# Another order around the seven value products of an attention layer

## The chip, the cores and the metric

The kernel runs on one core of a Trainium2 chip. The metric is the device time of one execution in microseconds (us). Times are compared by the median of several runs; the profile page shows one profiled execution. The engines are TensorE (PE, matmuls; its weight loads are listed as PEld), VectorE (DVE), ScalarE (ACT), GpSimd (POOL, which computes and also issues some DMAs) and SyncE (SP, which issues the others). Each engine works through its own queue in order and waits for semaphores of the others. SBUF is the memory that all engines read; PE writes its sums to PSUM, eight banks of 128 x 512 float32.

## The reference

A trunk of two layers over 512 tokens of width 1024. Layer 0 mixes tokens with a gated linear recurrence, layer 1 with stick-breaking attention; each mixer is followed by a SwiGLU block (FFN), and each part has a root-mean-square norm ahead of it. The part that matters here is the start of the attention layer:

```python
h = _rmsnorm(x, norm_mix_g[1])
qkv = (h @ w_qkv).reshape(bsz, s, 3, SB_HEADS, SB_HEAD_DIM)
...
z = einsum("bhqd,bhkd->bhqk", qb, k32) * scale
log_beta = log_sigmoid(z)
log_1m = where(mask, log_sigmoid(-z), 0.0)
suffix = cumsum(log_1m, reverse=True) - log_1m
wts = where(mask, exp(log_beta + suffix), 0.0)
out = einsum("bhqk,bhkd->bhqd", wts, v32)
```

All is float32. The kernel gets this precision from PE by splitting each operand into a rounded high part and a remainder (`h` and `l`) and adding three matmuls: high x high, high x low, low x high.

## The kernel before

**Layout.** `x` is held transposed: eight tiles `x[0..7]` of 128 features x 512 tokens. At the end of the first FFN block (lines 1023 to 1065) its result is turned back by PE in two halves (`back`), `take(m)` adds a turned tile to `x[m]` on DVE, and `gain(m)` makes the attention's operands `u[m] = (uh, ul)`: `x` times the norm's gain, cast on ACT, remainder on DVE (lines 425, 426). `gain` also squares `x[m]` on ACT and adds the square to `acc` (line 481): tiles 1 to 6 on POOL, tile 7 on DVE. The sum over features of `acc`, taken by PE, gives the norm's factor per token (`norm_rs1`, which ends in a small chain of ACT and DVE and writes a diagonal matrix); `norm_rs2` spreads it with PE over a 128 x 512 tile `rsB`. The factor is applied after the projections.

**The value projection** is one matrix product of 512 tokens x 1024 features by 1024 x 1024. It is cut in two along tokens, features and columns, and done with seven block products in place of eight, as in Strassen's scheme (Winograd's variant). `vprod(q, out, c)` (line 559) is one call of product `q`: half `c` of its k tiles, twelve matmuls of 512 columns into two banks. So a product is two calls, 24 matmuls. Products 1, 2 and 4 use `u` itself. Products 5 and 6 use sums made by `vops1(k)`, 7 and 3 sums made by `vops2(k)`, for k = 0 to 3: ACT scales two tiles of `x`, DVE makes sums of 256 columns, ACT casts the high part, DVE subtracts for the low part. Banks: `A` = 4 and 5, `B` = 2 and 3, `B2` = 0 and 1. Between products the banks are copied (ACT) or added (DVE) into `r1`, `u2`, `b5`, and `v_evac` writes value tiles `vs` from them: two ACT and two DVE instructions for each bank, ACT and DVE by turns.

**Weights** come as pieces of 512 KB in a fixed list; `VUnit.order` (line 79) says in which order the seven products' pieces and the first three q/k tiles of weights (`"k"`) stand in it. Each is split by `split_one()`: `wh` by ACT (line 329), `wl` by DVE or POOL (line 331; of the value stage, the list positions in `V_POOL` go to POOL). There are three buffers of `wh` and of `wl`, so a split waits for the matmuls of the third tile before it. `chunk()` hands the next piece to a product or a projection; ahead of that it issues loads on SP and runs `split_one()` until a set distance ahead of the use is reached, three pieces in the value stage. Pieces of products 6, 7 and 4 are not loaded: `plus` adds a second block to the buffer of an earlier piece (5, 3 and 6) with an accumulating DMA that POOL issues (line 101) at the next call of `chunk()` after that piece's split.

**Projections.** `proj(t, part)` is half of tile `t` of queries (even t) or keys (odd t), twelve matmuls. `proj_evac1` scales it on DVE by `rsB`; `proj_evac2` splits it, and for queries SP then copies it with eight DMAs into operands of two heads. `s1(h)` is the scores of head h into three banks (head 0: banks 0 to 2, head 1: banks 3 to 5). `chain_a(h)` follows: three ACT functions, two DVE and one POOL instruction for each of the three banks. `rsum` adds a few DVE steps, `s2(h)` adds the masked sums on PE, `chain_b` and `s3` end the head. From `h = 0` on a loop over heads mixes these with the remaining projections.

**Order.** In a `manual_schedule` block the instructions of PE, ACT, DVE and POOL run in the order in which the code traces them. The end of the FFN and the attention are two such blocks; where they meet, a scheduler interleaves them, and it also places the DMAs of SP. The order around the products before is in lines 1329 to 1397: products 1, 5, 3, 6, 2, 7, then scores and chain of head 0, then product 4.

## Time and profile before

| | |
|---|---|
| three runs | 1117.54, 1118.59, 1120.10 us; median 1118.59 |
| the profiled execution's own time | 1120.09 us |
| its span, first to last instruction | 1118.4 us |
| mean granted PE clock | 0.992 of full speed |
| seven value products, first to last matmul | about 492 to 567 us of the span |

The 1.7 us between span and time lie outside the program's instructions. Rows of a timeline read: start and length in us, engine, line, operation, output<-inputs by the program's names, count; in brackets how long the engine sat idle before it, and who ended the idle time. Matmul lengths overlap; what counts is the distance of their starts. A row with "x4" merges neighbours of one kind.

### The profile page before, as it was taken

What the parts mean: (1) busy time and instruction counts of PE and PEld (TensorE: products, weight loads), DVE (VectorE), ACT (ScalarE), POOL (GpSimd) and SP (SyncE); (2) the same over time, 40 slices, a digit from 0 to 9 for tenths busy, and PEclk for the clock granted to TensorE, in tenths of its full rate; (3) what the DMA queues carried; (4) which work ended last, traced back from release to release, by engine and by line L of the source; (5) the groups of instructions that cost most, each with busy time, mean ns of one, the idle gap of its engine ahead of it and who ended that gap; (6) DMA issues with size and microseconds to landing.
All of it is one profiled execution on the core that took longest, in us unless ns stands there. A gap on an engine that the chain in (4) does not pass through costs nothing.

```text
span 1118.4 us, 14779 instructions
## 1 busy us (share of the span) xinstructions
PE 1088.2 (97%) x5231; PEld 905.7 (81%) x5231; DVE 922.2 (82%) x1285; ACT 729.6 (65%) x1112; POOL 375.3 (34%) x283
## 2 busy tenths in 40 slices
PE   9999999999999999998889999999999999999997
PEld 6888888888888888876668888888887888888895
DVE  7977787777979799987778888978669797988897
ACT  6697677666555564646669999977764554646465
POOL 1652432324242414122434444422232415140412
PEclk9999999999999999999889999999999999999999
DMA  8532349977777765443853342224887767675432
GB/s 312 139 97 76 114 133 218 189 211 155 205 162 184 174 147 147 129 129 61 177 161 83 91 128 78 77 79 131 205 187 183 177 166 191 156 203 115 151 73 75
DMA packets 48537, 164.06 MB, mean 147 GB/s; under 512 B 5840, under 2 KB 6096, under 8 KB 48464
## 3 DMA queue, kind: packets, MB, share of 16 engines
q1 hardware_dynamic: 34640, 113.32, 31.1%
q0 software_dynamic: 13536, 49.29, 25.1%
q8 instruction: 41, 0.67, 0.2%
q10 hardware_dynamic: 288, 0.52, 0.1%
q14 instruction: 32, 0.26, 0.1%
HBM read 152.62 MB, written 2.10 MB: 138 GB/s over the span
## 4 chain that ended last, share of the span: by engine, by line
PE 67%; DVE 13%; ACT 6%; issue 4%; DMA 2%; DVEq 0%; POOL 0%; POOLq 0%; ACTq 0%
PE bank L793 15%; PE bank L794 15%; PE bank L795 15%; PE bank L369 5%; PE bank L367 5%; PE bank L368 5%; DVE wl L331 4%; PE bank L1240 2%; DMA bu<-w_gu 2%; DVE y L785 2%; PE bank L1266 1%; ACT wh L329 1%; PE bank L800 1%; PE bank L568 1%; ACT t L1204 1%
## 5 line engine op out<-in xcount | busy, mean ns | idle before, releaser
L329 ACT CAST wh<-raw 128x1024 fp32r<-128x1024 f32 x130 | 135.8, 1048 | 79.5 <-PE bank L795 34.5
L331 DVE TENSOR_TENSOR wl<-raw,wh 128x1024 fp32r<-128x1024 f32 x112 | 168.7, 1509 | 21.9 <-ACT wh L329 21.8
L793 PE MATMUL bank<-wh,ow 128*128 128x512 f32 (+1 forms) x480 | 179.7, 374 | 1.7 <-DVE b L785 1.7
L795 PE MATMUL bank<-wh,ow 128*128 128x512 f32 (+1 forms) x480 | 178.3, 372 | 0.0
L794 PE MATMUL bank<-wl,ow 128*128 128x512 f32 (+1 forms) x480 | 178.3, 371 | 0.0
L101 POOL DMA_DIRECT2D bu<-w_gu x64 | 56.2, 878 | 274.6 <-DMA bu<-w_gu 125.5
L329 ACT CAST wh<-bu 128x1024 fp32r<-128x1024 f32 x72 | 75.7, 1052 | 64.2 <-PE bank L795 38.3
L331 DVE TENSOR_TENSOR wl<-bu,wh 128x1024 fp32r<-128x1024 f32 x70 | 86.9, 1258 | 29.7 <-ACT wh L329 28.9
L793 PEld LDWEIGHTS bank<-wh,ow 128*128 128x128 f32 x480 | 90.4, 188 | 18.2 <-issue 2.9
L369 PE MATMUL bank<-uh,wl 128*128 128x512 f32 x256 | 100.6, 395 | 4.3 <-DVE wl L331 4.3
L367 PE MATMUL bank<-uh,wh 128*128 128x512 f32 x256 | 102.3, 402 | 2.2 <-ACT wh L677 1.0
L795 PEld LDWEIGHTS bank<-wh,ow 128*128 128x128 f32 x480 | 90.4, 188 | 15.7
L794 PEld LDWEIGHTS bank<-wl,ow 128*128 128x128 f32 x480 | 90.4, 188 | 15.3
L368 PE MATMUL bank<-ul,wh 128*128 128x512 f32 x256 | 100.5, 394 | 0.6 <-DVE ul L426 0.5
L785 DVE TENSOR_TENSOR y<-y,bank 128x512 f32<-128x512 f32 x140 | 88.9, 678 | 2.2 <-PE bank L795 2.1
L793 PE MATMUL bank<-wh,hth 128*128 128x512 f32 (+1 forms) x194 | 75.4, 389 | 0.0
L794 PE MATMUL bank<-wl,hth 128*128 128x512 f32 (+1 forms) x194 | 75.2, 387 | 0.0
L795 PE MATMUL bank<-wh,htl 128*128 128x512 f32 (+1 forms) x194 | 75.1, 387 | 0.0
L331 DVE TENSOR_TENSOR wl<-bv,wh 128x1024 fp32r<-128x1024 f32 x46 | 60.6, 1327 | 17.3 <-ACT wh L329 17.2
L331 POOL TENSOR_TENSOR wl<-raw,wh 128x1024 fp32r<-128x1024 f32 x20 | 50.8, 2543 | 69.6 <-ACT wh L329 57.9
L329 ACT CAST wh<-bv 128x1024 fp32r<-128x1024 f32 x48 | 49.7, 1048 | 22.4 <-PE bank L795 13.5
L369 PEld LDWEIGHTS bank<-uh,wl 128*128 128x128 f32 x256 | 48.6, 190 | 15.1 <-DVE wl L331 4.7
(309 smaller groups left out, 2811.7 us busy)
## 6 DMA issues: line engine op xcount, KB each, us to landing
bu<-w_gu POOLq DMA_DIRECT2D x64, 512.0 KB, 5.6
raw<-w_gu SPq DMA_DIRECT2D x44, 512.0 KB, 3.7
raw<-w_dn SPq DMA_DIRECT2D x24, 512.0 KB, 5.2
bu<-w_gu SPq DMA_DIRECT2D x22, 512.0 KB, 4.3
bv<-w_gu SPq DMA_DIRECT2D x22, 512.0 KB, 4.2
bv<-w_gu POOLq DMA_DIRECT2D x22, 512.0 KB, 6.7
d<-w_dn SPq DMA_DIRECT2D x20, 512.0 KB, 3.6
raw<-w_qk SPq DMA_DIRECT2D x16, 512.0 KB, 3.7
```

The lines of the kernel that those rows point to most:

```text
L101: kern.soon(lambda: kern.nc.gpsimd.dma_start(t, self.part(n), accum_op=ALU.add))
L329: (self.nc.vector.tensor_copy if self.wh_dve else self.nc.scalar.copy)(wh[:, c], raw)
L331: self.wli = self.wl_engine(i).tensor_tensor(wl[:, c], raw, wh[:, c].bitcast(F32), ALU.subtract)
L367: mm(out, lhsT=wh, rhs=xh, start=first, stop=False)
L368: mm(out, lhsT=wh, rhs=xl, start=False, stop=False)
L369: mm(out, lhsT=wl, rhs=xh, start=False, stop=last)
L568: mm(out[j], lhsT=oh[:, ts(j)], rhs=h, start=first and k == 0, stop=False, skip_group_check=True)
L785: add = lambda o, a, b: nc.vector.tensor_tensor(o, a, b, ALU.add)
L793: mm(out, lhsT=xh, rhs=wh, start=first, stop=False, skip_group_check=True)
L794: mm(out, lhsT=xh, rhs=wl, start=False, stop=False, skip_group_check=True)
L795: mm(out, lhsT=xl, rhs=wh, start=False, stop=last, skip_group_check=True)
L1240: mm(zt[kt][:, o0:o0 + ZW[j]], lhsT=tri if j == kt else one_n, rhs=s_, start=False, stop=True, skip_group_check=True)
```

## The change

- `gain` no longer squares. The squares of all eight tiles come behind product 5 (`squares`), and their adds are all on DVE. `norm_rs1` and `norm_rs2` move from around product 5 to around product 6's second call.
- Takes and gains 4 to 7 move from the FFN's block into the attention's block, takes by twos ahead of the gains.
- `vops1` and `vops2` become `scaled`, `ops1` and `ops2`: two k tiles at a time, halves and casts of both first, then both remainders. `ops2` makes the operands of product 3 and of product 7 apart; those of 7 come behind the squares. The full `vl`, `vh` pair of `vops2` becomes one tile per product and k.
- The distance of `chunk()` in the value stage becomes 1, and `split_one()` (`S_`) is called at chosen places. Products 2 and 7 change places in the list. POOL's positions are 12, 14 and 16: the second pieces of 7, 2 and 4.
- The evacuation of the three first projections comes behind the norm: `proj_evac1` for all three, one product call later `proj_evac2`.
- `v_evac` issues its two ACT instructions ahead of its two DVE instructions.
- Product 4's first call and the split of the fourth q/k tile come ahead of the scores and chain of head 0, which stay ahead of product 4's second call and of the last value tiles.

```diff
-V_POOL = (8, 10, 12, 14, 16)
+V_POOL = (12, 14, 16)
...
-        self.order = (1, "k", "k", "k", 5, 3, 6, 2, 7, 4)
+        self.order = (1, "k", "k", "k", 5, 3, 6, 7, 2, 4)
...
-        ahead = ahead or (4 if ffn else 3 if v else self.AHEAD_SPLIT)
+        ahead = ahead or (4 if ffn else 1 if v else self.AHEAD_SPLIT)
...
-                        self.norm_in(m, gnext)
+                        self.norm_in(m, gnext, False)
...
                 take(2, 3)
+                self.split_one()
                 self.vprod(1, self.bank[4:6], 0)
                 gain(2, 3)
+                self.split_one()
                 back(1)
                 self.vprod(1, self.bank[4:6], 1)
-                for m in range(4, KT):
-                    take(m)
-                    gain(m)
+                self.rest = take, gain
...
+                def scaled(k):
                     ua, ub, w1 = w[k] = [self.new("vw") for _ in range(3)]
                     nc.scalar.activation(ua, self.x[k], AF.Copy, scale=self.col("g_mix1", k))
                     nc.scalar.activation(ub, self.x[k + 4], AF.Copy, scale=self.col("g_mix1", k + 4))
...
+                def ops1(*ks):
+                    for k in ks:
+                        ua, ub, w1 = w[k]
+                        sub(w1[:, lo], ub[:, hi], ua[:, hi])
+                        nc.vector.scalar_tensor_tensor(w1[:, hi], w1[:, lo], -1.0, ua[:, lo], ALU.mult, ALU.subtract)
+                        h, l = self.new("vh", F32R), self.new("vl", F32R)
+                        nc.scalar.copy(h, w1)
+                        self.vops[k] = {5: (h[:, lo], l[:, lo]), 6: (h[:, hi], l[:, hi]), 1: (h, l)}
+                    for k in ks:
+                        h, l = self.vops[k][1]
+                        sub(l, w[k][2], h.bitcast(F32))
+
+                def ops2(q, *ks):
+                    for k in ks:
+                        ua, ub, w1 = w[k]
+                        hl = self.new("vx", F32R)
+                        if q == 3:
+                            o = ub[:, hi]
+                            nc.vector.scalar_tensor_tensor(o, ub[:, lo], -1.0, w1[:, hi], ALU.mult, ALU.subtract)
+                        else:
+                            o = ub[:, lo]
+                            sub(o, ua[:, lo], ua[:, hi])
+                        nc.scalar.copy(hl[:, lo], o)
+                        self.vops[k][q] = hl[:, lo], hl[:, hi]
+                        self.vops[k][-q] = o, hl
+                    for k in ks:
+                        h, l = self.vops[k][q]
+                        sub(l, self.vops[k][-q][0], h.bitcast(F32))
+                        if q == 7:
+                            self.rel(*w[k])
...
                         nc.scalar.activation(v[:, :, 0:64], pj, AF.Copy, scale=r)
+                    for j in range(2):
+                        v = vs[t][2 * half + j]
+                        pj = pvv[:, 4 * j:4 * j + 4, :]
                         nc.vector.scalar_tensor_tensor(v[:, :, 64:128], pj, r, v[:, :, 0:64].bitcast(F32),
                                                        ALU.mult, ALU.subtract)
...
+                def squares(*ms):
+                    for m in ms:
+                        self.norm_sq(m, nc.vector)
+
+                take(4)
+                take(5)
+                gain(4)
+                gain(5)
+                take(6)
+                take(7)
                 copies(r1, A)
+                gain(6)
+                gain(7)
                 pq = []
                 for t in range(2):
                     proj(t, 0)
                     pq.append((self.pt, self.pw))
-                    vops1(t)
+                S_()
+                scaled(0)
+                scaled(1)
+                ops1(0, 1)
                 for t in range(2):
                     self.pt, self.pw = pq[t]
                     proj(t, 1)
                 proj(2, 0, self.bank[0])
                 pq.append((self.pt, None))
-                vops1(2)
-                vops1(3)
+                S_()
+                scaled(2)
+                scaled(3)
+                ops1(2, 3)
+                S_()
                 proj(2, 1)
+                ops2(3, 0, 1)
+                self.vprod(5, B, 0)
+                S_()
+                ops2(3, 2, 3)
+                self.vprod(5, B, 1)
+                copies(b5, B)
+                S_()
+                squares(0, 1, 2, 3)
+                self.vprod(3, B, 0, False)
+                S_()
+                squares(4, 5, 6, 7)
+                self.vprod(3, B, 1, False)
+                ops2(7, 0, 1)
+                S_()
+                self.vprod(6, A, 0, False)
                 self.bi = 1
                 self.norm_rs1()
                 nc.vector.tensor_scalar(self.nrs, self.rsT, -1.0, None, ALU.mult)
                 nc.scalar.preload_act_table_set("natural_log_exp_and_others")
...
+                ops2(7, 2, 3)
+                S_()
+                self.vprod(6, A, 1, False)
...
+                copies(u2, A)
                 self.bi = 1
                 self.norm_rs2()
...
+                S_()
+                tts = []
+                for t in range(3):
                     self.pt = pq[t][0]
                     proj_evac1(t)
-                    proj_evac2(t)
...
+                    tts.append(self.tt)
                 for x, y in zip(u2, B):
                     add(x, x, y)
+                self.vprod(7, A, 0, False)
+                S_()
+                for t in range(3):
+                    self.tt = tts[t]
+                    proj_evac2(t)
+                self.vprod(7, A, 1, False)
+                self.rel(*(e[-7][1] for e in self.vops))
+                S_()
                 for t in range(2):
                     v_evac(t, 1, u2[t])
...
+                for x, y in zip(b5, A):
+                    add(x, x, y)
+                self.vprod(2, B2, 0)
+                S_()
+                for t in range(2):
+                    v_evac(2 + t, 1, b5[t])
+                self.vprod(2, B2, 1)
+                S_()
                 for x, y in zip(r1, B2):
                     add(x, x, y)
+                self.vprod(4, A, 0, False)
+                S_()
                 for t in range(2):
                     v_evac(t, 0, r1[t])
...
                 s1(0)
                 chain_a(0)
                 for i in range(3):
                     rsum(0, i)
-                for c in range(2):
-                    self.vprod(4, A, c, False)
+                self.vprod(4, A, 1, False)
                 for t in range(2):
                     v_evac(2 + t, 0, A[t])
                 self.wl_dve = False
```

More of the change, by code (lines that the diff above doesn't have):

```diff
@@ L1289, in attention @@
                 r1, u2, b5 = ([self.new(n) for _ in range(2)] for n in ("vr", "vu", "vb"))
-                self.vops, w = [None] * 4, [None] * 4
+                self.vops, w = [{} for _ in range(4)], [None] * 4
+                take, gain = self.rest
+                S_ = self.split_one
                 def copies(dst, src):
@@ L1294, in copies @@
                         nc.scalar.copy(x, y)
-                def vsplit(src):
-                    h, l = self.new("vh", F32R), self.new("vl", F32R)
-                    nc.scalar.copy(h, src)
-                    sub(l, src, h.bitcast(F32))
-                    return h, l
-                def vops1(k):
+                def scaled(k):
                     ua, ub, w1 = w[k] = [self.new("vw") for _ in range(3)]
@@ L1346, in attention @@
                 nc.scalar.preload_act_table_set("natural_log_exp_and_others")
-                vops2(0)
-                vops2(1)
-                self.vprod(5, B, 0)
+                ops2(7, 2, 3)
+                S_()
+                self.vprod(6, A, 1, False)
+                self.rel(*(t for e in self.vops for t in e[1]), *(e[-3][1] for e in self.vops))
+                copies(u2, A)
                 self.bi = 1
                 self.norm_rs2()
-                vops2(2)
-                vops2(3)
@@ L1354, in attention @@
-                self.vprod(5, B, 1)
-                copies(b5, B)
-                def proj_out(t):
+                S_()
+                tts = []
+                for t in range(3):
                     self.pt = pq[t][0]
                     proj_evac1(t)
-                    proj_evac2(t)
-                proj_out(0)
-                for c in range(2):
-                    self.vprod(3, B, c, False)
-                    proj_out(1 + c)
-                for c in range(2):
-                    self.vprod(6, A, c, False)
@@ L1368, in attention @@
-                self.rel(*(t for e in self.vops for t in e[1]))
-                copies(u2, A)
+                    tts.append(self.tt)
                 for x, y in zip(u2, B):
                     add(x, x, y)
+                self.vprod(7, A, 0, False)
[6 more added lines that the diff above has]
+                S_()
@@ L1372, in attention @@
                 for t in range(2):
                     v_evac(t, 1, u2[t])
-                self.rel(*u2)
-                for c in range(2):
-                    self.vprod(2, B2, c)
+                for x, y in zip(b5, A):
[6 more added lines that the diff above has]
+                S_()
                 for x, y in zip(r1, B2):
@@ L1378, in attention @@
                     add(x, x, y)
+                self.vprod(4, A, 0, False)
+                S_()
                 for t in range(2):
                     v_evac(t, 0, r1[t])
-                self.rel(*r1)
-                for c in range(2):
-                    self.vprod(7, A, c, False)
-                self.rel(*(t for e in self.vops for t in e[0]))
-                for x, y in zip(b5, A):
-                    add(x, x, y)
-                for t in range(2):
-                    v_evac(2 + t, 1, b5[t])
@@ L1389, in attention @@
-                self.rel(*b5)
+                self.rel(*u2, *r1, *b5)
                 s1(0)
@@ L1393, in attention @@
                     rsum(0, i)
-                for c in range(2):
-                    self.vprod(4, A, c, False)
+                self.vprod(4, A, 1, False)
                 for t in range(2):
```

11 lines of the change are left out of this document (removed).

## The prediction

> **What bounds the kernel now.** I read the page's busy line first, then the list of what TensorE (PE) waited for around the seven value products, then busy time in three stretches of that stage. The stretches run from the first value product to the last projection matmul (A), from there to the first scores (B), and from the first scores to the end of the second ones (C).
>
> ```profile
> PE 1088.2 (97%) x5231; PEld 905.7 (81%) x5231; DVE 922.2 (82%) x1285; ACT 729.6 (65%) x1112; POOL 375.3 (34%) x283
> ```
>
> ```profile
> PE bank L568 <- ACT vb L1294: 7.8, 1, 7.8
> PE bank L369 <- DVE wl L331: 4.3, 1, 4.3
> PE bank L507 <- DVE t L493: 1.3, 1, 1.3
> ```
>
> ```profile
> 492.06:519.60 27.54, 25.45 (x113) 19.26 (x112) 23.53 (x33) 20.47 (x31) 11.38 (x10) 1.00 0.32 79
> 519.60:560.31 40.71, 31.61 (x137) 25.61 (x136) 28.79 (x51) 25.46 (x39) 14.53 (x9) 0.92 0.66 144
> 560.31:579.22 18.91, 14.16 (x59) 10.67 (x58) 13.37 (x20) 10.24 (x21) 6.03 (x6) 0.82 0.73 216
> ```
>
> The last three rows give the stretch, its length, the busy time of PE, its weight loads, DVE (VectorE), ACT (ScalarE) and POOL (GpSimd), then the granted clock and the DMA's share. PE is busy 97% of the span, so elsewhere only matmuls cost time. This stage is the exception: two waits alone make 12.1 us, and in B and C the granted clock is 0.92 and 0.82. What PE would need there comes from its rows in order of time, picked here and below (start, length, engine, line; in brackets idle time and who ended it):
>
> ```profile
> 495.51 1.91 PE L1032 MATMUL bank<-x,y 128*128 128x128 f32 x16
> 497.18 0.48 PE L568 MATMUL bank<-wh,uh 128*128 128x512 f32 x1
> 528.23 0.39 PE L570 MATMUL bank<-wh,vl 128*128 128x512 f32 x1
> 536.45 0.79 PE L568 MATMUL bank<-wh,vh 128*128 128x512 f32 x1 [7.83 <-ACT vb L1294]
> 540.45 0.50 PE L568 MATMUL bank<-wh,vh 128*128 128x512 f32 x1
> 546.03 0.39 PE L568 MATMUL bank<-wh,vh 128*128 128x512 f32 x1
> 549.21 0.39 PE L570 MATMUL bank<-wh,vl 128*128 128x512 f32 x1
> 560.31 0.39 PE L1183 MATMUL bank<-qh,ks 128*128 128x512 f32 x1
> 561.75 0.48 PE L568 MATMUL bank<-wh,uh 128*128 128x512 f32 x1
> 572.95 0.80 PE L369 MATMUL bank<-uh,wl 128*128 128x512 f32 x1 [4.28 <-DVE wl L331]
> 579.22 0.48 PE L367 MATMUL bank<-uh,wh 128*128 128x512 f32 x1
> ```
>
> Fifteen matmuls start from 546.03 to 549.21: 0.227 us each, 2.72 for the twelve of one call of a product or of half a projection. A has 96 of them (21.8) and sixteen transposes (1.7, to 497.18): 23.5 of 27.5, so **4.0 lost**. B has ten calls (27.2) and the two norm sums, for which I allow 1.7: 28.9 of 40.7, **11.8 lost**. Most of that is the 8.0 from 528.46 to 536.45. Then nine matmuls take 4.00 (to 540.45) instead of 2.04: after the long wait the clock is halved, which costs **2.0**. C has first scores of 1.44 (560.31 to 561.75), two product calls, half a projection and second scores of 1.44: 11.0 of 18.9, **7.9 lost**.
>
> **Part A: operands and norm.** In these rows POOL adds squares while DVE makes two operands:
>
> ```profile
> 495.75 3.15 POOL L481 TENSOR_TENSOR acc<-acc,t 128x512 f32<-128x512 f32 x2 [0.87 <-ACT t L479]
> 495.98 3.47 DVE L426 SCALAR_TENSOR_TENSOR ul<-x,x,uh 128x512 fp32r<-128x512 f32 x2
> 502.05 0.75 DVE L426 SCALAR_TENSOR_TENSOR ul<-x,x,uh 128x512 fp32r<-128x512 f32 x1 [0.79 <-ACT uh L425]
> 509.71 0.61 ACT L479 ACTIVATE t<-x 128x512 f32<-128x512 f32 x1
> ```
>
> Two `ul` take 3.47, against 0.75 for one alone: 2.0 lost to POOL's adds. Each square also holds ACT 0.61, and operands of product 5 are made before the last two gains. The change takes the squares out and makes the gains first. With takes at 0.61, `ul` at 0.67 to 0.75 and a weight split at 1.2, DVE then ends the last `ul` at 504.3, and PE asks for it at about 507. I leave 0.7 (the first operands come as before): A takes 24.2, **3.3 saved**. The splits of the first two k tiles keep their place behind takes 2 and 3, so nothing new stands ahead of these operands.
>
> **Part B: what is removed.** The 8.0 wait is a chain, not work:
>
> ```profile
> 525.22 0.42 DVE L1313 SCALAR_TENSOR_TENSOR vw<-vw,vw 128x256 f32<-128x256 f32 x1
> 526.18 0.62 ACT L1298 CAST vh<-vw 128x512 fp32r<-128x512 f32 x1 [1.43 <-DVE vw L1287]
> 535.00 0.69 DVE L1287 TENSOR_TENSOR vl<-vw,vh 128x512 fp32r<-128x512 f32 x1 [0.74 <-ACT vh L1298]
> 535.82 1.06 ACT L1294 COPY vb<-bank 128x512 f32<-128x512 f32 x2
> ```
>
> For each of four k, DVE makes halves (0.42), ACT casts (0.62), DVE subtracts (0.69), each waiting for the other, four in line from 525.22 to 535.69. ACT's copy of the banks stands behind all of it, and product 3 needs that copy. The change makes two k together, so that one's cast lies beside the other's halves, and makes those of product 3 before the copy and those of product 7 later. The copy's first half then comes before product 5 ends (bank 0 is complete six matmuls earlier): no wait is left there, nor the 2.0 of slow clock. What is late next is DVE, which gets more work:
>
> ```profile
> 510.73 0.68 DVE L481 TENSOR_TENSOR acc<-acc,t 128x512 f32<-128x512 f32 x1
> 512.52 1.22 DVE L331 TENSOR_TENSOR wl<-bu,wh 128x1024 fp32r<-128x1024 f32 x1 [0.35 <-ACT wh L329]
> 535.99 2.38 POOL L331 TENSOR_TENSOR wl<-bv,wh 128x1024 fp32r<-128x1024 f32 x1 [3.53 <-ACT wh L329]
> ```
>
> Seven adds of squares at 0.6 (4.2; six were POOL's), and two more splits at 1.14 (2.3), since POOL keeps three of five. I lay the queues end to end with these durations, PE from 516.3. Product 5 and the first call of product 3 find all operands. Second call of 3: split ends 524.6, PE comes at 524.4 (0.1). Product 6: behind three adds DVE ends its split at 527.6, PE comes at 527.2 (0.3). Its second call: four adds (2.4), four pieces of product 7's operands (1.8), 0.5 for the cast, split (1.14): 533.6, PE comes at 531.1 after the first norm sum (2.3). Product 7: ACT has two table loads, two casts and a split before it copies A, done 538.4, DVE's split 539.2, PE comes at 537.2 (1.7). Its second call waits for POOL's split at 542.8 (0.8). Products 2 and 4 find theirs. That is 5.2, and 0.1 for each of some seven restarts. The norm's own wait of 1.3 is gone: the diagonal is ready at 535.6, under the second call of 6. I add 0.7, as durations laid end to end leave out collisions. B with eleven calls (29.9), sums (1.7) and 6.6 lost: 38.2 against 40.7, **2.5 saved**, though one call came over from C.
>
> What I cost at nothing: six accumulating transfers (`plus`) go out right behind the splits they follow,
>
> ```profile
> bu<-w_v POOLq DMA_DIRECT2D x4, 512.0 KB, 7.0
> 482.82 13.59 SPq L113 DMA_DIRECT2D raw<-w_v  x2
> ```
>
> 7.0 us each to landing. The tightest, for product 6's second half, goes out at 516 and is wanted at 531; without that cover each microsecond late is one of PE's. The load bound is one piece shorter, but product 2's raw pieces landed near 500 and are split past 543. The sixteen q copies move past four splits to about 541.8; the product calls to 554 hide them.
>
> **Part C: scores later.** Before, the wait for `wl` (4.3) hid a second limit:
>
> ```profile
> 566.59 0.89 POOL L101 DMA_DIRECT2D bu<-w_gu  x1 [0.32 <-issue]
> 569.35 1.32 POOL L1208 TENSOR_TENSOR spl<-sp,sph 128x384 fp32r<-128x384 f32 x1
> 567.92 3.05 DVE L1216 TENSOR_TENSOR t<-sp 128x256 f32<-128x256 f32 x1
> 571.33 0.42 DVE L1221 TENSOR_TENSOR r<-t,r 128x256 fp32r<-128x256 f32 x1
> 571.67 2.35 DVE L331 TENSOR_TENSOR wl<-raw,wh 128x1024 fp32r<-128x1024 f32 x2
> 576.38 0.48 DVE L1326 SCALAR_TENSOR_TENSOR vs<-bank,x,vs 128x256 fp32r<-128x256 f32 x1 [0.54 <-ACT vs L1325]
> ```
>
> The split of the next k tile (571.67) stood in DVE's queue behind the first head's chain. The change puts it ahead, so the 4.3 wait goes. But the second scores write banks 4 and 5, from which DVE takes the last value tiles, and those stay behind the chain: `rsum` ends 571.75, 10.0 after the first scores end. In those 10.0 are 2.6 in which L1216 stands behind POOL's subtractions (the third ends 570.67), late themselves by two transfers, of which the second ends 567.5. I keep the 10.0, for the same order remains. With T the start of the first scores, `rsum` ends at T+11.4 and the value tiles (0.45 each) free bank 4 at T+12.3 and bank 5 at T+13.2. PE has 1.4, one call and half a projection (5.4) and 0.5 of scores in bank 3: T+7.4. So it **waits 4.9**, then 0.5, and ends at T+13.8. Behind it on PE stand the next half projection and the first head's sums, and ACT's and DVE's chain of the second head waits for them. The wait removed was 4.3 and slowed the clock, so I count 2.0 for this one too: 15.8 against 18.9, **3.1 saved**, nearly all of it the call that B has taken.
>
> [...] The trace has both its long waits slow (4.3 and 7.8), and I stay with it.
>
> **Sum.** 3.3 + 2.5 + 3.1 = 8.9 off the profiled execution's 1120.09, which gives 1111.2; off the median of the three runs, 1118.59, which I predict, **1109.7**. Behind the second scores PE has no wait in the old trace, and I let the rest shift unchanged. Bounds of what the trace doesn't show: DVE's collisions in B from nothing (0.7 better) to the 2.0 of part A at each of POOL's three splits (5.3 worse); POOL's delay in C from nothing (2.6 better) to 10.0 as kept; the clock from 0 to 2.0. The likeliest case alone: 1107 to 1112.
>
> **Rivals.** *POOL clears C*: if the two transfers fall behind its subtractions, L1216 runs unblocked, 2.6 earlier; PE waits 2.3, short of the waits that slowed the clock: 4.6 better, **1105.1**. For it: in my layout only 3.8 us lie between POOL's last split (554.6), which frees the buffer that the second transfer needs, and the first operand for POOL (558.4). Against: the old order has as little there, and the transfers went first. *DVE bounds B*: it was busy 28.8 of 40.7; with 6.5 more it has 35.3 in 38.2. If the 5.3 above come true: **1115.0**. *The gain is handed back*: the second scores and the loop behind them wait for splits (the fourth k tile's is now behind the value tiles) as long as was saved: **1118.6**. Against: the old list of waits ends with these scores, and their own order of work is unchanged. *The q copies land late*, and the first scores wait:
>
> ```profile
> 540.09 3.20 SPq L1161 DMA_DIRECT2D qh<-qx  x2
> DMA to landing us min/median/max: 2.2/2.3/9.0
> 556.69 0.85 SPq L113 DMA_DIRECT2D bv<-w_gu  x2
> ```
>
> Before, SyncE's (SP) queue was so slow under the accumulating transfers that a pair of copies took 3.2, and one copy into `qh` landed after 9.0 (second row, smallest, middle and largest). In the new order SP has loads for the next FFN due at the same time, which wait for split buffers up to 554.6. If one stands ahead of the first head's four copies, these take 6.4 and 9.0 to land, 570.0 in all: 15.5 after the 554.5 at which the first scores are due, which is 6.6 over the 8.9 saved: **1125.2**. It decides from 8.9 late. Against: SP sent the copies ahead of those loads before (556.69). That the change doesn't do what it says is no case here: the order is fixed by hand on four engines.
>
> **Chances.** Forecast 0.50, POOL clears C 0.20, DVE bounds B 0.13, handed back 0.07, q copies late 0.10. Faster by over 0.2% (2.2 us, about what a measurement can tell from no change): 0.83; within: 0.07; slower: 0.10. The range runs from 1104.5 to 1115.5; it leaves out the last two cases and little more.
>
> **What would show it.** Right in A: no POOL adds before 520 and no wait of PE in the projections. Right in B: no wait over 2.5, the largest at product 6's second call or product 7, none on `vb`. Right in C: the wait on `wl` gone, and in its place one on the value tiles (L1326 of the old lines) before the second scores, of 2 to 5 us, with a slow clock behind it if long. A wait on `qh`, or one for the accumulated pieces on ACT, would make it wrong; so would new waits behind the second scores.

## The result, and the profile after

The changed kernel takes 1108.93 us (median of four runs, 1107.36 to 1111.86) where the kernel before, run beside it, took 1118.94 (1117.54 to 1120.1). The ratio is 0.9914, with a 95% interval of 0.989 to 0.9938. The prediction was 1109.7, faster. The profiled execution is the fastest of the four: 1107.36, its span 1105.6, which is 12.8 less than before. Medians here and below leave out two executions of hundreds of us more at a low granted clock, one of the kernel before (1547.26, clock 0.654) and one of run 7 (1813.87, clock 0.556). The busy line of the page of the profiled execution:

```profile
PE 1085.6 (98%) x5231; PEld 904.4 (82%) x5231; DVE 923.5 (84%) x1297; ACT 729.3 (66%) x1116; POOL 362.2 (33%) x275
```

PE's busy time fell by 2.6 only (1088.2 before; one matmul of 512 columns at half clock counts 0.63 and not 0.39, as the row at 536.00 below shows). The other 10.2 of the 12.8 is idle time, and the place of it shows in busy time by the three stretches A, B and C of the prediction (columns as there: the stretch, its length, PE, weight loads, DVE, ACT, POOL, granted clock, DMA):

```profile
492.18:516.44 24.26, 24.11 (x114) 19.57 (x112) 22.14 (x37) 17.92 (x27) 1.36 (x3) 1.00 0.33 88
516.44:556.34 39.90, 35.60 (x150) 27.36 (x148) 33.42 (x60) 29.07 (x49) 11.07 (x8) 0.96 0.73 148
556.34:567.81 11.47, 8.91 (x48) 6.96 (x46) 11.31 (x20) 10.01 (x21) 6.35 (x6) 1.00 0.75 238
```

A fell from 27.54 to 24.26, **3.3** as predicted. B fell from 40.71 to 39.90, **0.8** where 2.5 were predicted. C fell from 18.91 to 11.47, **7.4** where 3.1 were predicted. That is 11.5; behind C, from its end to the end of the span, another 1.4 went (539.2 to 537.8), and A began 0.1 later. So two errors of opposite sign met: B gave 1.7 less than the sum had, C 4.3 more. For the profiled executions the sum of 8.9 was 3.8 short, and the median, which fell by 10.0, came nearer to it than they did: that the number is close is luck in part. The list of what PE waited for (total, times, longest) shows what took the place of the old waits of 7.8 and 4.3:

```profile
PE bank L1183 <- DVE vs L1344: 2.6, 2, 2.4
PE bank L569 <- DVE wl L331: 2.2, 3, 1.2
...
PE bank L568 <- ACT wh L329: 1.0, 1, 1.0
PE bank L569 <- POOL wl L331: 0.8, 1, 0.8
...
PE bank L793 <- DVE b L785: 0.5, 2, 0.3
```

No wait is left on `vb` and none on the norm's diagonal. The first row is the one that the prediction named for C, on the value tiles (now line 1344), but half as long. The last row was 1.7 before: of its waits the longest, 1.24 at 854.76 in the second FFN, is gone, and that is most of what went behind C. Now the rows of B in order of time:

```profile
524.78 2.28 DVE L481 TENSOR_TENSOR acc<-acc,t 128x512 f32<-128x512 f32 x3
...
528.12 3.08 DVE L481 TENSOR_TENSOR acc<-acc,t 128x512 f32<-128x512 f32 x4
...
533.30 0.49 PE L568 MATMUL bank<-wh,vh 128*128 128x512 f32 x1 [1.00 <-ACT wh L329]
...
534.56 0.79 PE L569 MATMUL bank<-wl,vh 128*128 128x512 f32 x1 [0.77 <-DVE wl L331]
...
536.00 0.63 PE L569 MATMUL bank<-wl,vh 128*128 128x512 f32 x1
...
541.40 2.41 POOL L331 TENSOR_TENSOR wl<-bv,wh 128x1024 fp32r<-128x1024 f32 x1 [5.67 <-ACT wh L329]
...
543.86 0.50 PE L569 MATMUL bank<-wl,vx 128*128 128x512 f32 x1 [0.80 <-POOL wl L331]
...
545.52 3.50 DVE L1169 TENSOR_TENSOR ks<-t,ks 64x512 fp32r<-64x512 f32 x2
...
553.72 0.50 PE L569 MATMUL bank<-wl,uh 128*128 128x512 f32 x1 [1.17 <-DVE wl L331]
```

Read them as one queue. The seven adds of squares take 5.4 (first two rows), and behind them product 6's second call gets its `wh` and `wl` 1.0 and 0.8 late and runs at 0.427 per matmul (a row at 536.00 lasts 0.63, not 0.39), product 7's second call waits for POOL's split, and product 4's first call waits 1.17, which the prediction did not have. And C:

```profile
561.54 2.28 POOL L1208 TENSOR_TENSOR spl<-t,sph 128x512 fp32r<-128x512 f32 x2 [4.02 <-DVE sph L1207]
...
563.36 0.75 DVE L1216 TENSOR_TENSOR t<-sp 128x256 f32<-128x256 f32 x1
...
564.90 1.80 POOL L101 DMA_DIRECT2D bu<-w_gu  x2
...
565.14 0.42 DVE L1221 TENSOR_TENSOR r<-t,r 128x256 fp32r<-128x256 f32 x1
...
566.41 0.44 PE L1183 MATMUL bank<-qh,ks 128*128 128x384 f32 x1 [2.39 <-DVE vs L1344]
```

POOL subtracts first and issues its two transfers (line 101) behind that; before, they stood ahead. So L1216 takes 0.75 and not 3.05, the first head's sums (`rsum`, last DVE instruction L1221) end 9.2 after the first scores and not 11.4, PE waits 2.39 for the value tiles, and the clock stays full (1.00 in C).

### The profile page after: what moved, and what is told of

Same layout as the page of the kernel before. It is cut to its first block, busy times and chain, and to the rows that moved or that the text cites. A ratio compares the mean times of both kernels' runs of the same rounds, so it can differ in the third digit from the quotient of the medians.

```text
span 1105.6 us, 14788 instructions
## 1 busy us (share of the span) xinstructions
PE 1085.6 (98%) x5231; PEld 904.4 (82%) x5231; DVE 923.5 (84%) x1297; ACT 729.3 (66%) x1116; POOL 362.2 (33%) x275
## 4 chain that ended last, share of the span: by engine, by line
PE 73%; DVE 11%; ACT 5%; issue 3%; DVEq 0%; ACTq 0%
PE bank L793 17%; PE bank L794 17%; PE bank L795 17%; PE bank L367 5%; PE bank L369 5%; PE bank L368 5%; DVE wl L331 3%; PE bank L1240 2%; DVE y L785 1%; PE bank L800 1%; PE bank L1266 1%; ACT t L1204 1%; ACT wh L329 1%; DVE ks L1169 1%; ACT t L1203 1%
## 5 line engine op out<-in xcount | busy, mean ns | idle before, releaser
L1208 POOL TENSOR_TENSOR spl<-t,sph 128x512 fp32r<-128x512 f32 (+1 forms) x32 | 39.1, 1243 | 57.5 <-DVE sph L1207 55.5
```

Of the source, the lines that this page charges most:

```text
L1208: nc.gpsimd.tensor_tensor(sl[:, w], sp[:, w], sh[:, w].bitcast(F32), ALU.subtract)
```

## The experiments

Twelve kernels ran, each the changed kernel with the edit named. Times are medians beside the kernel before, whose medians in the three sets of runs were 1118.9, 1119.1 and 1118.9. A, B, C and "behind" (from the end of C to the end of the span) are of each one's profiled execution, with the boundaries used above.

| kernel | A | B | C | behind | median | ratio to before, 95% |
|---|---|---|---|---|---|---|
| before | 27.5 | 40.7 | 18.9 | 539.2 | 1118.94 | |
| changed | 24.3 | 39.9 | 11.5 | 537.8 | 1108.93 | 0.9914 [0.989, 0.9938] |
| 1 POOL late | 24.3 | 40.0 | 13.1 | 539.1 | 1111.21 | 0.9931 [0.9911, 0.995] |
| 2 value tiles first | 24.3 | 40.0 | 8.4 | 540.6 | 1107.26 | 0.9892 [0.9871, 0.9912] |
| 3 split of 6 first | 24.3 | 39.9 | 11.9 | 538.9 | 1108.95 | 0.9906 [0.9887, 0.9924] |
| 4 product 2's split on DVE | 24.3 | 39.0 | 11.9 | 538.9 | 1107.6 | 0.9904 [0.9878, 0.993] |
| 5 squares back in A | 25.8 | 38.5 | 11.4 | 537.8 | 1108.79 | 0.9907 [0.9892, 0.9922] |
| 6 split behind the chain | 24.3 | 40.9 | 15.5 | 537.8 | 1112.03 | 0.9936 [0.9921, 0.9951] |
| 7 fill, behind the sums | 24.3 | 41.5 | 12.0 | 538.8 | 1111.95 | 0.9934 [0.9917, 0.9951] |
| 8 = 2 and 4 | 24.3 | 39.0 | 8.4 | 538.0 | 1104.32 | 0.9869 [0.9852, 0.9885] |
| 9 fill, ahead of the sums | 24.3 | 39.7 | 11.8 | 539.2 | 1108.22 | 0.9905 [0.9887, 0.9923] |
| 10 product 7's operands early | 24.3 | 38.1 | 12.0 | 538.9 | 1108.2 | 0.9903 [0.9885, 0.992] |
| 11 one k tile at a time | 24.3 | 44.8 | 11.9 | 538.6 | 1113.62 | 0.995 [0.9933, 0.9966] |
| 12 = 8, and 7's between the copies | 24.3 | 36.6 | 8.4 | 537.8 | 1101.37 | 0.9839 [0.9822, 0.9855] |

A began between 491.7 and 493.7, though nothing was edited ahead of it. Differences of spans under 2 us therefore mean little; the lengths of the stretches are what to compare. These move too: B is 40.9 in run 6, where nothing in it was edited, and C runs from 11.4 to 12.0 where nothing in it was edited. Only the intervals of runs 8 and 12 lie apart from that of the changed kernel, so for the others the waits in the rows carry the argument and the time goes beside them.

### What C hangs on: runs 1, 6 and 2

Run 1 puts two subtractions whose result is not used ahead of POOL's first one in the first head's chain:

```diff
+                    if h == 0 and i == 0:
+                        dum = self.new("dum")
+                        for _ in range(2):
+                            nc.gpsimd.tensor_tensor(dum, sp, sh.bitcast(F32), ALU.subtract)
+                        self.rel(dum)
                     nc.gpsimd.tensor_tensor(sl[:, w], sp[:, w], sh[:, w].bitcast(F32), ALU.subtract)
```

> Edit: two extra POOL subtractions of 128x512 (1.3 us each) that read the first head's first sph, ahead of POOL's own ones. Theory (POOL's place sets stage C: L1216 of rsum stands behind POOL's subtractions, the value tiles behind rsum, the second scores behind the value tiles): rsum ends about 3 us later, PE's wait before the second scores grows from 2.4 to 5 to 5.5, the clock is halved behind it, C takes 16 to 17 us in place of 11.5, the whole 4 to 5.5 us more. Rival (DVE's own work sets it, POOL is beside it): C stays at 11.5, the time within 1 us.

Rows of its timeline, the added work, the wait of the second scores (line 1344 is 1349 here) and the first matmul behind them:

```profile
561.72 2.67 POOL L1211 TENSOR_TENSOR dum<-t,sph 128x512 f32<-128x512 f32 x2 [4.01 <-DVE sph L1207]
...
567.93 0.44 PE L1183 MATMUL bank<-qh,ks 128*128 128x384 f32 x1 [3.70 <-DVE vs L1349]
...
569.68 0.78 PE L367 MATMUL bank<-uh,wh 128*128 128x512 f32 x1
```

2.7 more on POOL make PE's wait 3.70 in place of 2.39, and the matmul behind it lasts 0.78 and not 0.48 (the granted clock is 0.58 from 568.4 to 571.8); C and what is behind it get 1.6 and 1.3 longer, the time 2.3. DVE's three steps of `rsum` take 1.11, 1.24 and 1.10 there and 0.75, 0.97 and 0.42 in the changed kernel: DVE waits for nothing, but POOL's subtractions now run beside all three (POOL is busy for all 3.40 from 565.0 to 568.4). So POOL's work does move the end of C, though half of an added microsecond is absorbed: the theory held in kind, with C at 13.1 and not the 16 to 17 expected. No run puts the two transfers themselves ahead again; that they alone made the old 3.05 is read from the rows and not shown by a run.

Run 6 moves the split of the fourth q/k tile back to where it was before the change:

```diff
                 self.vprod(4, A, 0, False)
-                S_()
                 for t in range(2):
...
                     rsum(0, i)
+                S_()
                 self.vprod(4, A, 1, False)
```

> Undoes one part: the split of the fourth q/k tile stands behind the first head's chain and sums again, as before the change. Theory (its place was worth the old wait on wl): PE asks for it at 560.6 and DVE ends it behind rsum at about 566, so a wait of 4 to 5.5 on wl or wh comes back ahead of the half projection, with a slow clock behind it; the wait of 2.4 for the value tiles goes. C goes from 11.5 to 15 to 17, the time to 1112 to 1114.5. Rival (the value tiles behind the chain set the end of C either way): C stays under 13 and the time under 1110.

```profile
564.35 0.79 PE L367 MATMUL bank<-uh,wh 128*128 128x512 f32 x1 [2.59 <-ACT wh L329]
...
567.41 0.79 PE L369 MATMUL bank<-uh,wl 128*128 128x512 f32 x1 [1.85 <-DVE wl L331]
```

The two rows are the waits that come back ahead of the half projection: 2.59 for `wh` and 1.85 for `wl`, 4.4 together, as long as the old one, with slow matmuls behind (0.63 each up to 570.57, 0.40 from 570.87 on). C is 15.5, the value tiles are no longer waited for. B's 1.0 more, where nothing was edited, goes with a slow stretch that lasted to 539.4 there and not 537.7. The place of this one split is worth 4 us of C and about 3 us in the medians.

Run 2 puts the last value tiles ahead of the third part of the chain:

```diff
-                chain_a(0)
-                for i in range(3):
-                    rsum(0, i)
+                chain_a(0, (0, 1))
                 self.vprod(4, A, 1, False)
                 for t in range(2):
                     v_evac(2 + t, 0, A[t])
+                chain_a(0, (2,))
+                for i in range(3):
+                    rsum(0, i)
```

> Edit: the last value tiles go ahead of the third bank's chain and of rsum on ACT and DVE. Theory (what is left in C is the value tiles' place in DVE's queue): the wait of 2.4 before the second scores falls under 0.7, C takes 9 to 9.7 in place of 11.5, and the first head's sums, which need rsum, still don't wait. Rival (rsum becomes the bound itself): the 2 us come back as a wait of PE before L1240.

C is 8.42, which is PE's own work without a wait, and less than the 9 to 9.7 of the theory. But only 1.7 us came through in the median: behind C 2.8 were given back, as the rival had it, though at another place. DVE's rows show where, with the POOL instruction beside them:

```profile
571.57 3.02 DVE L1169 TENSOR_TENSOR ks<-t,ks 64x512 fp32r<-64x512 f32 x2
...
575.75 2.36 POOL L331 TENSOR_TENSOR wl<-raw,wh 128x1024 fp32r<-128x1024 f32 x1 [2.43 <-ACT wh L329]
...
576.04 2.22 DVE L1219 CAST r<-t 128x256 fp32r<-128x256 f32 x1
...
578.78 0.38 PE L1183 MATMUL bank<-qh,ks 128*128 128x256 f32 x1 [1.99 <-DVE awl L1255]
```

A cast of 256 columns (L1219) takes 2.22, and it starts under POOL's split (575.75 to 578.11); `awl` stands behind it in DVE's queue, and PE waits 1.99 for `awl`. In run 8 DVE reaches the same cast 1.1 us earlier, ahead of POOL's split (at 575.60), and it takes 0.28. Most of the 1.1 comes from two key remainders ahead of it (L1169), which take 3.02 in run 2 and 2.10 in run 8; POOL was subtracting beside them in both:

```profile
571.41 2.10 DVE L1169 TENSOR_TENSOR ks<-t,ks 64x512 fp32r<-64x512 f32 x2
...
574.96 0.28 DVE L1219 CAST r<-t 128x256 fp32r<-128x256 f32 x1
```

### What B hangs on: runs 4, 3, 7 and 9

Run 4 gives the second piece of product 2 to DVE:

```diff
-V_POOL = (12, 14, 16)
+V_POOL = (12, 16)
```

> Edit: the split of product 2's second piece is on DVE in place of POOL. Theory (the wait of 1.2 at product 4's first call comes from two key casts of DVE that stand 2 us behind POOL's split): L1169 x2 falls from 3.5 to 1.4, the wait of 1.2 falls under 0.5, B gets 0.7 to 1.2 shorter. Rival (DVE just has too much to do there): with 1.14 more for DVE the wait stays or grows.

```profile
545.13 1.40 DVE L1169 TENSOR_TENSOR ks<-t,ks 64x512 fp32r<-64x512 f32 x2
...
552.36 0.50 PE L569 MATMUL bank<-wl,uh 128*128 128x512 f32 x1 [0.40 <-DVE wl L331]
```

The two key remainders (L1169) take 1.40 and not 3.50, and product 4's first call waits 0.40 and not 1.17: B is 0.9 shorter, as the theory had it, although DVE has one split more to do. Most of the wait that the prediction had missed came from POOL's split running beside DVE's two-operand instructions.

Run 3 calls the split for product 6's second call ahead of product 7's operands, and not behind them:

```diff
-                ops2(7, 0, 1)
                 S_()
+                ops2(7, 0, 1)
                 self.vprod(6, A, 0, False)
```

> Edit: the split of product 6's second piece goes ahead of the first operands of product 7. Theory (B's loss is that split's place behind operands that nobody needs yet, and the halved clock behind it comes from PE's sparse work there, not from one long wait): the waits of 1.0 and 0.8 at the second call of 6 fall under 0.3, the clock stays full, B takes 36.5 to 37 in place of 39.9, the whole 2.5 to 3.5 less. Rival A (the norm's small matmuls alone halve the clock): the waits go but about 1.5 of slow clock stays: B 38 to 38.5. Rival B (DVE's sum of work sets it): the wait moves to product 7, B stays over 39.

```profile
PE bank L568 <- ACT vu L1296: 2.0, 1, 2.0
...
PE bank L507 <- DVE t L493: 1.1, 1, 1.1
```

The waits of 1.0 and 0.8 are gone, and in their place stand 2.0 for the copy of banks 4 and 5 and 1.1 for the norm's diagonal, ahead of product 7. The slow stretch moved as well: it lies at 539.4 to 542.8 (granted clock 0.52), in product 7's first call. B is unchanged: rival B. Product 7 can't start earlier than the queue of ACT and DVE lets it.

Was the half clock of product 6's second call a loss, then? Runs 7 and 9 fill the time in which PE had little to do with five matmuls whose results are not used, run 7 behind the norm sums (448 columns), run 9 ahead of them. This is the edit of run 9:

```diff
                 self.bi = 1
+                for _ in range(5):
+                    nc.tensor.matmul(self.bank[1], lhsT=self.u[4][0][:, 0:P], rhs=self.u[5][0], start=True, stop=True)
                 self.norm_rs1()
```

> Adds five matmuls of 448 columns (about 1 us in all, into unused columns of the norm's bank) between the norm sums and product 6's second call, where PE waits 1.0 us for wh. Their results are not used. Theory (the clock of 534.4 to 537.8 is halved because PE was busy only 1.6 of the 3.4 us before, while what bounds this place is the ACT and DVE queue up to the split of product 7's first piece, done at 540.0): the matmuls of product 6's second call run 0.227 apart, and PE waits 1.2 to 1.8 more for product 7's wl or for the copy of bank A: B stays at 40 within 0.4, the time at 1107 to 1109. Rival 1 (the slow clock is what B lost): B falls by 1.3 to 1.6, no new wait. Rival 2 (the clock doesn't hang on how busy PE was there): still 0.427 apart, B as it is or 0.2 longer.

Run 7 failed as an experiment: the added matmuls write the bank of the norm sums and had to wait 2.8 for ACT and DVE to read these, so PE stood idle longer. It tells one thing: product 6's second call began 3.9 later than in the changed kernel, and B grew by 1.6 only.

> As the run that filled the window, with the five matmuls (512 columns, 1.1 us, into the norm's bank, results not used) ahead of the norm sums, where they wait for nothing: the sums then end at 533.4, just when PE gets wh for product 6's second call. Theory (the clock of a stretch of about 3.4 us is set by how busy PE was in the one before, and what bounds B here is the ACT and DVE queue up to product 7's split): PE is busy 2.7 and not 1.6 of 531.0 to 534.4, product 6's second call runs at full clock and ends 1.5 earlier, and PE then waits 1.2 to 1.6 more ahead of product 7: B within 0.4 of 40.3, time 1107 to 1109.5. Rival 1: the slow clock is what B lost: B 38.7 to 39, 1106 to 1107.5. Rival 2: the clock doesn't hang on that: matmuls still 0.427 apart.

Run 9 does what run 7 was meant to. Busy time in 3.4 us around the start of product 6's second call (its first matmul is the last of the first stretch in the changed kernel) and in the 3.4 us behind, first of the changed kernel, then of run 9:

```profile
531.00:534.40 3.40, 1.59 (x10) 1.15 (x9) 2.75 (x6) 2.82 (x4) 0.00 (x0) 1.00 0.72 136
534.40:537.80 3.40, 3.24 (x8) 2.56 (x9) 2.77 (x14) 2.46 (x6) 0.86 (x1) 0.50 0.44 53
```

```profile
531.00:534.40 3.40, 3.13 (x19) 2.65 (x17) 2.68 (x6) 1.68 (x3) 0.00 (x0) 1.00 0.99 152
534.40:537.80 3.40, 2.57 (x10) 1.90 (x11) 2.87 (x12) 2.84 (x4) 0.86 (x1) 1.00 0.22 27
```

PE was busy 1.59 in the first stretch of the changed kernel and the clock of the second is 0.50; with 3.13 it is 1.00. The slow clock is gone, and B is 39.7 in place of 39.9: just below the 39.9 to 40.7 of the theory, and far from the 38.7 to 39 of rival 1. PE waits 0.99 and 0.28 ahead of product 7 for what it no longer loses. The slow clock that ended before the next operand was there cost next to nothing, 0.2. The one that lasted longer did cost: in run 6 it lasted 1.7 longer, and B grew by 1.0.

### The operands: runs 5, 10 and 11

Run 5 lets `gain` square again, with six adds on POOL, and empties `squares`:

```diff
-                        self.norm_in(m, gnext, False)
+                        self.norm_in(m, gnext)
...
-                    for m in ms:
-                        self.norm_sq(m, nc.vector)
+                    pass
```

> Undoes one part: the squares go back into the gains, where POOL adds six of them, and the list of squares behind product 5 is empty; all else as in the changed kernel. Theory (POOL's adds stretch DVE's two-operand instructions in A, and DVE's adds are what makes B late): A goes from 23.8 to 26.5 to 27, POOL adds stand in A again with pairs of ul near 3.4, DVE is busy 4 us less in B, the waits of product 6's second call (1.0 and 0.8) go, and B falls from 40.3 to 37 to 39, so that the whole is within 2 us of the changed kernel's 1107 to 1109. Rival 1 (the order of takes and gains alone made A shorter): A stays under 24.5 and the whole is 2 to 3 us faster. Rival 2 (DVE's adds don't bound B): A 27, B 40, 3 us slower.

```profile
496.64 3.47 DVE L426 SCALAR_TENSOR_TENSOR ul<-x,x,uh 128x512 fp32r<-128x512 f32 x2
...
526.08 0.50 PE L568 MATMUL bank<-wh,vx 128*128 128x512 f32 x1 [1.97 <-ACT vb L1296]
```

The pair of `ul` takes 3.47 again, A is 1.5 longer and not 3, B 1.4 shorter, and the median is the same within 0.2: moving the squares shifted 1.5 us from A to B and gained nothing by itself. In B the copy is late for product 3 (1.97) instead. The other 1.8 of A's saving came with the other edits there, the order of takes and gains among them; no run takes these apart.

Run 10 makes all of product 7's operands ahead of the copy of banks 2 and 3, as before the change, but by pairs:

```diff
+                ops2(7, 0, 1)
                 ops2(3, 2, 3)
+                ops2(7, 2, 3)
                 self.vprod(5, B, 1)
...
-                ops2(7, 0, 1)
...
-                ops2(7, 2, 3)
```

> Undoes one part: product 7's operands are made before the copy of banks 2 and 3 again, now by pairs (those of the first two k tiles ahead of product 3's second pair, the others behind it). Theory (what removed most of the wait of 7.8 was the work by pairs, the place gave the rest): the copy comes 2 to 3 us later and PE waits 2 to 2.8 for vb ahead of product 3, not 7.8; in return the waits of product 6's second call (1.0 and 0.8) go and product 7 starts earlier: B 39.5 to 41.5, time 1107.5 to 1110. Rival (the place was what mattered): a wait of 5 or more with a slow clock behind it, B over 43, time over 1112.

```profile
525.62 0.50 PE L568 MATMUL bank<-wh,vx 128*128 128x512 f32 x1 [2.08 <-ACT vb L1296]
```

The wait on `vb` is 2.08, not 7.8, and B is 1.8 shorter than in the changed kernel: product 6's second call no longer waits and no matmul of B runs slow, as product 7's operands are off DVE's queue by then. So the long wait goes without the place behind the squares too, and that place cost B more than it gave. (In the median 0.7 came through; C and what is behind it got 1.6 longer, with matmuls of 0.63 behind the second scores.)

Run 11 undoes the pairs:

```diff
-                ops1(0, 1)
+                ops1(0)
+                ops1(1)
```

and so at the other five places.

> Undoes one part: the six places make the operands of one k tile after the other (halves, cast and remainder, then the next), as before the change, and not two side by side. Theory (each place gets about 1 us longer as DVE waits for the cast): products 5, 3, 6 and 7 each find theirs 0.5 to 1.3 later, A or B has 2 to 3 us more, time 1110.5 to 1112. Rival (other work fills DVE's gaps and the pairs are worth nothing once 7's operands are away from the copy): within 0.7 of the changed kernel, 1108 to 1109.6.

```profile
525.24 0.50 PE L568 MATMUL bank<-wh,vx 128*128 128x512 f32 x1 [3.06 <-ACT vb L1296]
...
537.20 0.75 PE L568 MATMUL bank<-wh,vh 128*128 128x512 f32 x1 [1.89 <-ACT wh L329]
```

3.06 for the copy, 1.89 for product 6's `wh`, and a slow clock to about 543 (the last matmul of 0.63 starts at 542.89): B is 4.9 longer, the time 4.7, nearly half of what the whole change gained, and more than the 2 to 3 us expected. A is unchanged, since product 5's operands had slack. No other part that was undone costs as much. But of the old wait of 7.8 only 3.06 comes back: the place of product 7's operands, which is kept here, holds back the rest. Pairs alone (run 10) or the place alone (run 11) each remove most of that wait; no run undoes both.

### A faster version: runs 8 and 12

Run 8 has the edits of runs 2 and 4 together.

> Two edits of before together: the last value tiles ahead of the third part of the first head's chain and of its sums, and the second piece of product 2 split by DVE and not by POOL. Theory (two separate waits): product 4's first call waits 0.4 and not 1.17, the second scores don't wait, no slow clock in C; B 39.4, C 8.5 to 9, and 1106 to 1107, the fastest so far. Rival (what PE gains there it waits for later, at the masked sums, as the 2.0 on awl in the run with the value tiles first): same as that run within 0.5, 1107 to 1107.8, with the wait on awl grown to 2.5 to 3.3.

1104.32: 1.7 below the 1106 to 1107 of the theory. The wait of 1.99 on `awl` of run 2 didn't come (the row at 574.96 above), and what is behind C is 2.6 shorter than in run 2. Run 12 adds one edit: the operands of product 7's first two k tiles go between the two copies of banks 2 and 3.

```diff
-                copies(b5, B)
+                nc.scalar.copy(b5[0], B[0])
+                ops2(7, 0, 1)
+                nc.scalar.copy(b5[1], B[1])
...
-                ops2(7, 0, 1)
```

> The run with both edits (value tiles first, second piece of 2 on DVE) and a third: the operands of product 7's first two k tiles are made between the two copies of banks 2 and 3, where ACT waits 0.77 for PE and DVE 2.7 for ACT, and not behind the squares. Theory (B is bounded by the queue of DVE and ACT behind the squares): product 6's second call finds wh and wl, the norm's chain and product 7 come 2 us earlier; B 36.8 to 37.8, time 1101.5 to 1102.7. Rival (the norm's chain and the copy of banks 4 and 5 bound product 7 in any case, as in the run with the split ahead): the waits of 1.0 and 0.8 move ahead of product 7, B over 39, time 1104 to 1104.6.

Its stages, in the view used for the others:

```profile
493.56:517.86 24.30, 24.15 (x114) 19.57 (x113) 22.18 (x37) 17.96 (x27) 1.41 (x3) 1.00 0.34 88
517.86:554.42 36.56, 33.77 (x149) 26.24 (x148) 32.34 (x62) 28.89 (x49) 8.19 (x7) 1.00 0.81 155
554.42:562.84 8.42, 8.42 (x47) 6.93 (x46) 8.42 (x16) 8.23 (x19) 3.40 (x3) 1.00 0.95 325
```

The clock is 1.00 throughout, B is 36.6 and C is PE's work alone. The longest wait left in B is this row of the timeline:

```profile
538.46 0.50 PE L568 MATMUL bank<-wh,vx 128*128 128x512 f32 x1 [0.98 <-ACT vu L1296]
```

That is 0.98 for ACT's copy of banks 4 and 5, ahead of product 7. 1101.37 us, 7.6 below the changed kernel, and their intervals lie apart.

## Why the prediction was right

The direction and the range held, and so did the causes of the two long waits. The terms did not all hold, and the total is near because errors of opposite sign met.

**A** (3.3 saved, 3.28 measured): right in size. Its reasons were right in kind: the pair of `ul` lost its 2.0 to POOL's adds (run 5 brings the 3.47 back). It named the squares and the order of the gains without saying what each gives; run 5 puts 1.5 on the squares. It did not see that B would pay back all that they gave.

**B** (2.5 saved, 0.8 measured): the long wait went by the mechanism given, a chain of ACT and DVE made by pairs and without product 7's operands ahead of the copy. Either part alone removes most of it (2.08 is left with the pairs alone, 3.06 with the place alone), and the pairs are worth more to the whole (4.7, run 11), as what stands behind the copy comes late without them too. The place itself cost 1.8 of B (run 10), since it puts those operands into the queue behind the squares. Two terms were off. "Seven adds of squares at 0.6", 4.2 in all, was mis-sized, though the prediction's own row for one add has 0.68: they took 2.28 + 3.08 = 5.4, so the operands behind them came about 1 us late, product 7's second call at 543.9 and not 542.8; of that the 0.7 allowed for collisions had covered a part. And the step "Products 2 and 4 find theirs" failed: POOL's split of product 2's second piece stretched DVE's key remainders to 3.50 (1.40 without it), and product 4's first call waited 1.17 (run 4). The half clock, which the prediction didn't have here either, cost about 0.2 (run 9). The waits it did forecast came in other places than listed (0.3 and not 1.7 ahead of product 7), as PE was late itself by then.

**C** (3.1 saved, 7.4 measured): the exchange of the 4.3 wait for one on the value tiles happened, and run 6 brings the old one back. The step that failed is "I keep the 10.0, for the same order remains": POOL's two transfers fell behind its subtractions, which the prediction had as the rival "POOL clears C" at 0.20, with a wait of 2.3 (measured 2.39) and C 4.6 shorter than forecast (measured 4.3). Run 1 shows that C's end follows POOL's work, though not one for one. The 2.0 of slow clock did not appear in the profiled execution. The lower bound of 0 for it was the author's estimate, and the runs show both cases: six other kernels with the same wait had slow matmuls behind it (below).

**Behind C**, "I let the rest shift unchanged" was 1.4 too cautious.

**The other rivals**: DVE bounded B in part; of the 2.0 that this rival put on each of POOL's three splits, one came in full (3.50 in place of 1.40), and PE lost 0.8 by it (run 4). The q copies were never waited for; nothing was handed back behind C. What the profiled execution gained beyond the median (12.7 against 10.0) stays open. In six kernels with the same 2.4 wait before the second scores (runs 3, 4, 7, 9, 10, 11) the clock halved behind it (matmuls of 0.63, not 0.39), and C and the rest together were about 1.5 longer than in the changed kernel's profile and run 5, where it did not. That could explain a part of the slowest of the four executions, 1111.86, whose granted clock was 0.993 against 0.996 in the profiled one. It does not explain the other two, 1108.46 and 1109.4: their clock was 0.997.

## What to carry over

Where two engines hand one operand back and forth, lay the chains of two operands side by side before looking at which instruction is slow: here undoing that cost 4.7 us, and moving the squares from POOL to DVE gave about nothing. A wait that is removed shows the next one in the same queue, so price the queue up to the next operand that PE needs (here product 7's) and not the single wait; where an engine idles on a hand-over, as ACT did between two copies, is the place for work that is late elsewhere. And before an instruction stream is taken as "unchanged", check on which side of it the DMA issues of the same engine will stand.

## What the runs showed of the hardware

**In these traces the granted clock of a stretch of about 3.41 us went with how busy PE was in the stretch before.** The slow clock lasts from 534.40 to 537.81 in the changed kernel's profile, 3.41; in that of the kernel before it lasts from 533.86 to 540.68 and from 571.40 to 578.23, two such stretches each time, with 30.72 of full clock between, which is nine. A wait of 2.4 halved the clock in run 4 and not in the changed kernel. The stretches of run 4 that end and begin at the change of the clock, and those of the changed kernel counted on in steps of 3.41 from its earlier slow stretch:

```profile
561.90:565.30 3.40, 1.03 (x6) 0.60 (x5) 3.33 (x8) 3.29 (x6) 3.40 (x4) 1.00 0.47 145
565.30:568.70 3.40, 3.31 (x12) 2.61 (x12) 2.79 (x5) 1.54 (x4) 0.55 (x2) 0.52 0.92 169
```

```profile
561.70:565.10 3.40, 2.31 (x11) 1.60 (x10) 3.27 (x6) 3.37 (x8) 3.40 (x4) 1.00 0.71 286
565.10:568.50 3.40, 1.93 (x11) 1.52 (x12) 3.37 (x8) 1.93 (x4) 1.60 (x2) 1.00 0.62 90
```

In run 4 the whole wait lies in one stretch: PE busy 1.03 of 3.4, the next one at 0.52. In the changed kernel it is cut in two: busy 2.31 and 1.93, and the clock stays full (1.00, also from 568.5 to 571.9). No sharp limit shows: 1.59 of 3.4, nearly half, had a slow stretch behind it in the changed kernel, 1.58 in the kernel before (527.03 to 530.44) had none, and 1.88 there (571.40 to 574.82, itself at half clock) had another slow one. So a wait well under 3.4 us brought a slow stretch here, and whether the same wait did differed from one kernel to the next.

**POOL beside DVE.** One cast (L1219) took 0.28 in run 8, ahead of POOL's split, and 2.22 in run 2, under it; a pair of remainders (L1169) took 1.40 in run 4 without POOL's split and 3.50 in the changed kernel beside it (545.62 to 548.48). The remainders have two inputs and the cast one; why DVE takes longer there no run shows.
